# A squared-ReLU MLP in an encoder block: another order of units and column halves in the second product

## The chip, the cores and the metric

The kernel runs on one core of one Trainium2 chip. The metric is the device time of one execution in microseconds. Matrix work is done by TensorE (PE, with PEld for the loading of its stationary operand), elementwise work by VectorE (DVE) and ScalarE (ACT); GpSimd (POOL) has next to nothing to do here, and SyncE (SP) issues the transfers. PE writes into eight accumulation banks of 128 x 512 fp32 (PSUM).

## The reference

One encoder layer on 256 tokens of width 2048: an attention mixer, a cross-attention on 256 memory tokens, and an MLP of inner width 8192, each followed by a residual sum and a layer norm. Only the MLP is touched:

```python
def squared_relu_mlp(h, w_mlp_in, w_mlp_out):
    return jnp.square(jax.nn.relu(h @ w_mlp_in)) @ w_mlp_out

ff = squared_relu_mlp(x, w_mlp_in[l], w_mlp_out[l])
x = layer_norm(ALPHA * x + ff, ln3_g[l], ln3_b[l])
```

All of it is fp32. The kernel gets that precision from matmuls on two reduced halves of each operand: a number is split into hi and lo, and a product a*b is made as hi*hi + hi*lo + lo*hi, three matmuls (`mm3`).

## The kernel before, in words

**Chunks, tiles, units.** The inner width of 8192 is cut into four chunks c of 2048, and a chunk into 16 columns of 128. A *column tile* ("g", c, j) makes one column of 128 of the first product: 16 matmuls of 512 columns and 16 of 256 into one bank (`hidden_tile`). Its bank is then emptied (`evacuate`), and two tiles j, j+1 together form a pair p, which is squared and split into hi and lo in `ht` (`stages`). A *unit* ("u", c, q, p) multiplies pair p of chunk c with the rows of w_mlp_out that belong to it, for the column half q (1024 of 2048 columns), for both blocks of 128 tokens.

**Two kinds of units.** A unit is a 2 x 2 by 2 x 2 block product. A plain one takes eight block products, 24 matmuls of 512 columns, into the banks x11, x12, x21, x22. A unit in seven products (`sevens`) uses a Strassen-like scheme: 21 matmuls into p1, p5, p6, p7 and x11, x12, x21. For it DVE makes three sums of weight blocks into `s_t` (`push_sums`), and each pair's hidden values need sums as well (`add`, `halve_sums` in `stages`; kept in `aux`). x22 is free meanwhile and takes the tiles between such units. Each 1024 columns of weights (or of sums) are split by one copy on ACT and one subtraction on DVE (`part`); hi and lo have four buffers each.

**Passes.** A pass (c, q) is eight units. The passes run (0,0), (0,1), (1,0), (1,1) and so on; units 0 to 5 of each are in seven products, 6 and 7 plain, and the last pass is plain throughout. The four last units of the kernel are "held": their first token block is multiplied at once, the second after all weights have been split. The tiles of the second half of a chunk stand between the units of its first pass, the first half of the next chunk between those of its second pass, one tile ahead of each unit (two at one place). After the last seven-product unit of a pass p1, p5, p6, p7 are added into the residual `res` by way of `m_t`, and at its end x11, x12, x21, x22: 12 merges of 512 columns on DVE a pass (`merge`, `more`).

**What sets the order.** Matmuls, splits, sums and some other rows are recorded through `queue`, which makes each follow the one before on its engine. The merges and most of a pair's conversion are free rows, placed between them by a scheduler at build time. `after(n, ...)` hangs work behind the n-th coming split. The rows of ln2's gain and bias are applied to the residual by `norm_ops`: the first half of the columns beside the start of the chunk, the second half from the second pass on. Weights come in 1 MB loads through a ring of four buffers; from the load JOIN on `row_b`, which held those rows, is the fifth.

Lines that the prediction names: L962 and L961 are the split of 1024 columns on DVE and ACT (L958, L957 after the change), L954 the sums into `s_t`, L877 the emptying of a tile's bank, L881, L900, L903 and L904 the conversion of a pair, L1215 the norm rows (L1229 after), L1113, L1114 and L1117 the merges (L1118, L1119, L1122 after), L164 to L166 the three matmuls of `mm3`, L1035 and L1043 those of a tile (L1028, L1036 after), L1191 the last merges (L1205 after), L1254 and L1262 the output rows (L1266, L1274 after).

Of the kernel before, what the change touches and what calls it, by code (L numbers as in the profile page):

```python
# [18 lines left out]
P = 128  # L19
# [19 lines left out]
def encoder_kernel(ctx: ExitStack, tc: tile.TileContext, t, out):  # L39
# [808 lines left out]
    ht_x = aux[:, 0:1024].rearrange("p (k c) -> p k c", c=512)  # L848
    sums_h = [aux[:, o:o + 1024] for o in range(1024, 8192, 1024)]
# [5 lines left out]

    place, free = {}, {"h": list(range(SLOTS)), "s": list(range(len(SEVEN) + 1))}

# [6 lines left out]
    def hid(c, p):  # L864
        i = 2 * place["h", c, p]
        return ht[:, i:i + 2, :] if i < CH else ht_x[:, i - CH:i - CH + 2, :]
# [16 lines left out]
    def stages(h, c, p, to=free_order):  # L883

        a11, a21, a12, a22 = [h[:, o:o + P] for o in range(0, 4 * P, P)]
        s = []

        def square():
            to(nc.scalar.activation(h, h, AF.Relu))
            to(nc.scalar.activation(h, h, AF.Square))  # L890

        def halve():
            take("h", c, p)
            x = hid(c, p)
            ordered_split(x[:, :, 0:S], x[:, :, S:2 * S], h.rearrange("p (i c) -> p i c", c=S), to)

        def add():
            s.append(tmp_tile())
            s3, s1, s2, s4 = [s[0][:, o:o + P] for o in range(0, 4 * P, P)]
            to(nc.vector.tensor_tensor(out=s[0][:, 0:2 * P].rearrange("p (i c) -> p i c", c=P),  # L900
                                       in0=a21[:, None, :].broadcast_to([P, 2, P]),
                                       in1=h.rearrange("p (i c) -> p i c", c=P)[:, 0:4:3, :], op=ALU.subtract))
            to(nc.vector.tensor_tensor(out=s2, in0=s1, in1=a11, op=ALU.subtract))  # L903
# [7 lines left out]
        return [square, halve] + [add, halve_sums] * (p in SEVEN)  # L911

    raws, raw_of, fetched, sums = [raw_x], {}, [0], deque()
    items = []
    for c, q in PASSES:
        us = [("u", c, q, p) for p in ORDER]
        gs = [("g", c, j) for j in range(LEAD, CH)] if q == 0 else [
            ("g", c + 1, j) for j in range(LEAD) if c < NCH - 1]
        for u in us:
            n = 2 if q == 0 and u[3] == (CH // 2 - 2 if c else 0) else 1  # L920
            items += gs[:n] + [u]
            gs = gs[n:]
    JOIN = items.index(("u", 0, 1, 7))
# [92 lines left out]
    def both(*todo):  # L1016
        return [lambda: [x() for x in todo]]

    now, late_finish, later, count = [], [], [], [0]
# [7 lines left out]
    def hidden_tile(it, ps):  # L1027
# [23 lines left out]
        if first:  # L1051
            after(4, lambda: evacuate(ps, h, j % 2, queue))
        else:
            evacuate(ps, h, j % 2)
        if j % 2 and first:
            square, halve, add, halve_sums = stages(h, c, j // 2, queue)
            n = 11 if j == LEAD + 1 else 5
            after(n, square)
            after(n + 2, add, halve)
            after(n + 3, halve_sums)  # L1060
        elif j % 2:
            def rest():
                for stage in stages(h, c, j // 2, queue if j == CH - 1 else free_order):
                    stage()
            late_finish.append(rest)

    at = [0]

    def step():
# [3 lines left out]
        if it[0] == "g" and late_finish:  # L1073
            late_finish.pop()()
# [13 lines left out]
    def one_pass(c, q):  # L1088

        order, sevens = ORDER, SEVENS[c, q]  # L1090
        final = (c, q) == PASSES[-1]
# [3 lines left out]
        left = {id(ps): len(sevens) * (ps is not x22) + 2 * (len(order) - len(sevens)) for ps in xs}  # L1095
        left.update({id(ps): len(sevens) for ps in pt})
        left[id(x22)] -= 2 * HELD * final
        total = dict(left)
# [5 lines left out]

        cols = [slice((2 * q + i) * 512, (2 * q + i + 1) * 512) for i in range(2)]
        r11, r12, r21, r22 = [res[b][:, cc] for b in range(NB) for cc in cols]

        fresh = [r11, r12, r21, r22] if c == 0 else []
# [10 lines left out]
        spare, n_seven, n_unit, parts = [], 0, 0, []  # L1119
        while n_unit < len(order):  # L1120
            it = step()
            if it[0] == "g":  # L1122
                if n_unit == 0:
                    ps = {LEAD: x22, LEAD + 1: x21}[it[2]] if it[1] == 0 else p6
                elif n_seven < len(sevens):
                    ps = x22
                else:
                    spare = spare or [p1, p6]
                    ps = spare[0]
                    spare.reverse()  # L1130
                hidden_tile(it, ps)
# [3 lines left out]
            if p in sevens:  # L1135
                if n_seven == 0:
# [10 lines left out]
                n_seven += 1  # L1147
                if at[0] < len(items) and is_seven(items[at[0]]):
                    push_sums(items[at[0]])
                if n_seven == len(sevens):  # L1150
                    nc.scalar.activation(m_t, p1, AF.Copy)

                    banks.extend([lambda: merge(r11, m_t), lambda: more(p6),
                                  lambda: merge(r12, m_t, ALU.subtract), lambda: more(p7, ALU.subtract),
                                  lambda: merge(r21, m_t), lambda: merge(r22, m_t, ALU.subtract),
                                  lambda: merge(r22, p5), lambda: merge(r12, p5)])
            elif final and len(order) - n_unit < HELD:
                n = len(parts) // 2
                for i in range(2):
                    o = (2 * n + i) * 1024  # L1160
                    lo = sums_h[2 * n + i - 1] if n + i else lo_tile()
# [4 lines left out]
            else:  # L1166
                for i in range(2):
# [4 lines left out]
            if q == 1:  # L1172
                give("h", c, p)
                if p in SEVEN:
                    give("s", c, p)
            if late_finish:
                late_finish.pop()()
        if not final:
            for r, ps in ((r22, x22), (r12, x12), (r11, x11), (r21, x21)):
                merge(r, ps)  # L1180
            if c == NCH - 1:
                xs[:], pt[:] = pt[:], xs[:]
                banks.extend([lambda b=b, r=r: stats(sts[b], r)
                              for b, r in ((0, r11), (0, r12), (1, r21), (1, r22))])
            return
# [33 lines left out]
    for g in range(LEAD // G):  # L1219
# [4 lines left out]
        if g == 0:  # L1224
            norm_rows(0)
            rows = norm_ops(0)
            (a1, a2, a3, a4), (b1, b2, b3, b4) = first, second
            side.extend(wait * 4 + empty + [a1, b1, a3, a2, a4, b3] + both(b2, rows[0])
                        + both(b4, rows[1]) + rows[2:])  # L1229
# [153 lines left out]
```

## Time and profile before

| | |
|---|---|
| median of 3 runs | 1097.57 us (1096.83 to 1098.71) |
| the profiled execution's own time | 1098.32 us |
| its span (first to last instruction) | 1096.5 us |
| matmuls on PE | 5846 |
| first column tile of the queued part | 446.1 us |
| last matmul | ends at about 1085.5 us |

All rows are of this one execution. A row of a timeline gives start, duration, engine, line, operation, tiles and shape; behind it in brackets the idle time before it and what ended that. Durations overlap: an engine begins the next row before the last has drained, so the step from start to start is what a row costs on a full engine. Rows of windows give the stretch, its length, and for PE, PEld, DVE, ACT and POOL the busy time and the count; then the granted PE clock (1.00 is full), the share of the transfers and their GB/s. A row of waits gives who waited for whom, total us, times, longest us.

### The profile page before, as it was taken

The numbers are of one execution on the slowest core, as the hardware profiler recorded it, in microseconds if no ns is written. First come the engines' busy times: TensorE is split into PE (matmuls) and PEld (weight loads), VectorE is DVE, ScalarE is ACT, GpSimd is POOL, SyncE is SP. The second block draws the span as 40 slices with busy tenths as digits, with TensorE's granted clock in tenths as the row PEclk, the third lists the DMA queues.
The fourth block names the chain that finished last, engine by engine and source line by source line (L and its number), as shares of the span: only waits on it lengthen the run. The fifth ranks groups of instructions, "written<-read, shape, count | busy, mean of one in ns | idle before, by whom it ended". The sixth has DMA issues, their size and how long they took to land.

```text
span 1096.5 us, 15253 instructions
## 1 busy us (share of the span) xinstructions
PE 1076.7 (98%) x5846; PEld 928.8 (85%) x5846; DVE 938.7 (86%) x1301; ACT 642.3 (59%) x937; POOL 36.2 (3%) x43
## 2 busy tenths in 40 slices
PE   9999999999999999999999999999999999999995
PEld 6988899988999878878888888888888888888885
DVE  6878678778889677999999999899999899999876
ACT  6555567555576426656566557466566566666640
POOL 2402000000000000000000000000000000000000
PEclk9999999999999999999999999999999999999998
DMA  9664454466577334555556555646556555655732
GB/s 327 246 227 136 156 189 157 156 228 238 182 216 267 143 128 176 209 192 198 191 202 244 202 188 199 216 170 226 198 186 225 198 192 198 224 175 195 253 145 78
DMA packets 37369, 215.87 MB, mean 197 GB/s; under 512 B 4272, under 2 KB 5168, under 8 KB 13616
## 3 DMA queue, kind: packets, MB, share of 16 engines
q1 hardware_dynamic: 37296, 214.89, 55.5%
q8 instruction: 46, 0.75, 0.3%
q14 instruction: 27, 0.22, 0.1%
HBM read 212.78 MB, written 2.10 MB: 196 GB/s over the span
## 4 chain that ended last, share of the span: by engine, by line
PE 92%; DVE 6%; issue 1%; ACT 1%; DMA 1%; SPq 0%; POOL 0%; DVEq 0%; ACTq 0%
PE acc L164 12%; PE acc L165 12%; PE acc L166 12%; PE acc L1035 11%; PE att L1035 6%; PE acc L1043 6%; PE att L165 5%; PE att L166 5%; PE att L164 5%; PE att L1043 3%; PE acc L206 2%; PE acc L204 2%; PE acc L205 2%; DVE lo L962 2%; PE acc L213 1%; PE att L213 1%
## 5 line engine op out<-in xcount | busy, mean ns | idle before, releaser
L87 ACT ACTIVATE w_hi<-raw 128x1024 fp32r<-128x1024 f32 (+2 forms) x134 | 131.6, 989 | 108.5 <-PE acc L166 73.9
L88 DVE TENSOR_TENSOR w_lo<-raw,w_hi 128x1024 fp32r<-128x1024 f32 (+2 forms) x130 | 147.2, 1142 | 50.3 <-ACT w_hi L87 49.2
L962 DVE TENSOR_TENSOR lo<-raw,w_hi 128x1024 fp32r<-128x1024 f32 (+1 forms) x156 | 173.0, 1128 | 9.2 <-ACT w_hi L961 9.0
L961 ACT ACTIVATE w_hi<-raw 128x1024 fp32r<-128x1024 f32 (+1 forms) x156 | 149.3, 980 | 25.5 <-PE acc L166 15.0
L1035 PE MATMUL acc<-x2t,w_hi 128*128 128x512 f32 x592 | 153.3, 391 | 0.0
L1035 PEld LDWEIGHTS acc<-x2t,w_hi 128*128 128x128 f32 x592 | 108.9, 189 | 19.6
L962 DVE TENSOR_TENSOR lo<-s_t,w_hi 128x1024 fp32r<-128x1024 f32 x84 | 102.4, 1222 | 10.8 <-ACT w_hi L961 10.7
L961 ACT ACTIVATE w_hi<-s_t 128x1024 fp32r<-128x1024 f32 x84 | 88.6, 1057 | 37.3 <-PE acc L1035 18.4
L1043 PEld LDWEIGHTS acc<-x2t,lo 128*128 128x128 f32 x592 | 80.8, 190 | 5.8
L1043 PE MATMUL acc<-x2t,lo 128*128 128x256 f32 x592 | 82.5, 282 | 0.0
L1035 PE MATMUL att<-x2t,w_hi 128*128 128x512 f32 x304 | 78.4, 391 | 0.0
L165 PE MATMUL acc<-lo,ht 128*128 128x512 f32 (+1 forms) x188 | 73.0, 389 | 1.1 <-DVE lo L962 1.1
L164 PE MATMUL acc<-w_hi,ht 128*128 128x512 f32 x186 | 72.5, 390 | 0.0
L166 PE MATMUL acc<-w_hi,ht 128*128 128x512 f32 x186 | 72.4, 389 | 0.0
L876 ACT ACTIVATE tmp<-acc 128x256 f32<-128x256 f32 x41 | 15.4, 384 | 92.2 <-PE acc L1035 87.9
L165 PE MATMUL acc<-w_lo,xt 128*128 128x512 f32 (+2 forms) x192 | 69.3, 362 | 0.0
L166 PE MATMUL acc<-w_hi,xt 128*128 128x512 f32 (+2 forms) x192 | 69.2, 361 | 0.0
L164 PE MATMUL acc<-w_hi,xt 128*128 128x512 f32 (+2 forms) x192 | 65.6, 361 | 1.2 <-ACT w_hi L87 1.2
L1035 PEld LDWEIGHTS att<-x2t,w_hi 128*128 128x128 f32 x304 | 55.8, 189 | 10.0
L962 DVE TENSOR_TENSOR lo<-raw_x,w_hi 128x1024 fp32r<-128x1024 f32 (+1 forms) x50 | 55.4, 1124 | 0.6 <-ACT w_hi L961 0.4
L165 PE MATMUL att<-lo,aux 128*128 128x512 f32 x139 | 54.4, 391 | 1.4 <-DVE lo L962 1.4
L164 PE MATMUL att<-w_hi,aux 128*128 128x512 f32 x139 | 54.1, 390 | 0.0
(287 smaller groups left out, 2513.1 us busy)
## 6 DMA issues: line engine op xcount, KB each, us to landing
raw<-in_w_mo SPq DMA_DIRECT2D x39, 1024.0 KB, 4.8
raw<-in_w_mc SPq DMA_DIRECT2D x37, 1024.0 KB, 4.8
raw<-in_w_out SPq DMA_DIRECT2D x16, 1024.0 KB, 4.9
raw_x<-in_w_mo SPq DMA_DIRECT2D x14, 1024.0 KB, 4.8
raw_x<-in_w_mc SPq DMA_DIRECT2D x12, 1024.0 KB, 4.8
row_b<-in_w_mo SPq DMA_DIRECT2D x11, 1024.0 KB, 4.8
raw<-in_w_mi SPq DMA_DIRECT2D x8, 1024.0 KB, 4.8
row_b<-in_w_mc SPq DMA_DIRECT2D x7, 1024.0 KB, 4.8
```

Of the source, the lines that this page charges most:

```text
L87: pin(nc.scalar.activation(hi, src, AF.Copy), pinned)
L88: return pin(nc.vector.tensor_tensor(out=lo, in0=src, in1=f(hi), op=ALU.subtract), pinned)
L164: keep(nc.tensor.matmul(ps, ah, bh, start=start, stop=False))
L165: keep(nc.tensor.matmul(ps, ah, bl, start=False, stop=False))
L166: keep(nc.tensor.matmul(ps, al, bh, start=False, stop=stop))
L204: nc.tensor.matmul(ps, hi, xt[:, k, 0:S], start=k == 0, stop=False)
L205: nc.tensor.matmul(ps, hi, xt[:, k, S:2 * S], start=False, stop=False)
L206: nc.tensor.matmul(ps, lo, xt[:, k, 0:S], start=False, stop=k == nk - 1)
L961: queue(nc.scalar.activation(hi, src, AF.Copy))
L962: queue(nc.vector.tensor_tensor(out=lo, in0=src, in1=f(hi), op=ALU.subtract))
L1035: queue(nc.tensor.matmul(ps, hi[:, k * P:(k + 1) * P], x2t[:, k0 + k, :], start=k0 + k == 0, stop=k0 + k == KT - 1))
L1043: queue(nc.tensor.matmul(ps[:, 0:S], lo[:, k * P:(k + 1) * P], x2t[:, k0 + k, 0:S], start=False, stop=False))
```

## The change

The passes now run (0,0), (0,1), (1,1), (1,0), (2,0), (2,1), (3,1), (3,0): half 0, then two passes of half 1, two of half 0, two of half 1, and half 0. Two passes that follow each other on one half keep all their banks, and the merges come once for both. A table (`UNITS`) says which units are plain ("P") or in seven products ("S"), `ORDERS` in which order the pairs come, `TILES` how many column tiles stand before each unit. Plain units stand at the outer ends of such a double pass; there are 48 S and 16 P units (42 and 22 before). The first pass begins with four tiles around two plain units; after that one tile stands before each unit but two, none in the last pass, and the tiles run two further ahead than before. `ht` has eight places for pairs instead of nine, `aux` eight for sums instead of seven, and a pair is converted when a place is free (`finish`). Tiles between plain units take p1, p6 or p7 (`tile_bank`). The second half of the norm rows is applied in the first pass, and `row_b` joins the ring of weights earlier.

The first place is DVE from the third split of the column tiles on (lo_4182, lo_4183, lo_4180, lo_4181 are the four lo buffers). Before:

```order
L962 TENSOR_TENSOR lo_4182<-raw,w_hi 128x1024
L954 TENSOR_TENSOR s_t<-raw 128x1024
L962 TENSOR_TENSOR lo_4183<-raw,w_hi 128x1024
L954 TENSOR_TENSOR s_t<-s_t,raw 128x512 x2
L962 TENSOR_TENSOR lo_4180<-raw,w_hi 128x1024
L962 TENSOR_TENSOR lo_4181<-raw,w_hi 128x512
L900 TENSOR_TENSOR tmp<-tmp 128x256
L903 TENSOR_TENSOR tmp<-tmp 128x128
L904 TENSOR_TENSOR tmp<-tmp 128x128
L881 TENSOR_TENSOR ht<-tmp,ht 128x2x256
L877 TENSOR_TENSOR tmp<-acc,tmp 128x256
L962 TENSOR_TENSOR lo_4182<-s_t,w_hi 128x1024
```

And now:

```order
L958 TENSOR_TENSOR lo_4182<-raw,w_hi 128x1024
L958 TENSOR_TENSOR lo_4183<-raw,w_hi 128x1024
L958 TENSOR_TENSOR lo_4180<-raw,w_hi 128x1024
L877 TENSOR_TENSOR tmp<-acc,tmp 128x256
L958 TENSOR_TENSOR lo_4181<-raw,w_hi 128x1024
L900 TENSOR_TENSOR tmp<-tmp 128x256
L903 TENSOR_TENSOR tmp<-tmp 128x128
L904 TENSOR_TENSOR tmp<-tmp 128x128
L881 TENSOR_TENSOR ht<-tmp,ht 128x2x256
L1229 TENSOR_TENSOR res_1484<-res_1484,row_b 128x1024
L958 TENSOR_TENSOR lo_4182<-raw,w_hi 128x1024
L881 TENSOR_TENSOR aux<-tmp,aux 128x512
```

The sums of weight blocks (L954) have left this place, since the first two units are plain; a norm row (L1229) has come.

The second place is DVE where the second pass ends and the third begins. Before (res is the residual, att and acc are banks):

```order
L962 TENSOR_TENSOR lo_4181<-raw,w_hi 128x1024
L1113 SCALAR_TENSOR_TENSOR res_1485<-res_1485,m_t 128x512 x2
L962 TENSOR_TENSOR lo_4182<-row_b,w_hi 128x1024
L881 TENSOR_TENSOR aux<-tmp,aux 128x512
L1114 TENSOR_TENSOR res_1485<-res_1485,att 128x512
L1114 TENSOR_TENSOR res_1484<-res_1484,att 128x512
L962 TENSOR_TENSOR lo_4183<-row_b,w_hi 128x1024
L962 TENSOR_TENSOR lo_4180<-raw,w_hi 128x1024
L954 TENSOR_TENSOR s_t<-raw_x 128x1024
```

And now:

```order
L958 TENSOR_TENSOR lo_4183<-s_t,w_hi 128x1024
L958 TENSOR_TENSOR lo_4180<-raw,w_hi 128x1024
L950 TENSOR_TENSOR s_t<-raw 128x1024
L958 TENSOR_TENSOR lo_4181<-raw,w_hi 128x1024
L900 TENSOR_TENSOR tmp<-tmp 128x256
L950 TENSOR_TENSOR s_t<-s_t,raw 128x512
L881 TENSOR_TENSOR ht<-tmp,ht 128x2x256
L903 TENSOR_TENSOR tmp<-tmp 128x128
L950 TENSOR_TENSOR s_t<-s_t,raw 128x512
```

The merges are gone from here; the seven-product units of both passes follow each other, with one tile between (rows two to four and six to nine belong to a tile and the next unit's sums).

The third place is DVE at the end, from the last merge on. Before:

```order
L1191 TENSOR_TENSOR res_1485<-res_1485,acc 128x256
L524 BN_STATS bn<-res_1485 128x6 x2
L1191 TENSOR_TENSOR res_1485<-res_1485,acc 128x256
L524 BN_STATS bn<-res_1485 128x6
L528 BN_AGGR mv<-bn 128x2
```

And now:

```order
L1274 SCALAR_TENSOR_TENSOR res_1484<-res_1484,rs_r,raw 128x256
L524 BN_STATS bn<-res_1485 128x6
L1205 TENSOR_TENSOR res_1485<-res_1485,acc 128x256
L1274 SCALAR_TENSOR_TENSOR res_1484<-res_1484,rs_r,raw 128x256
L524 BN_STATS bn<-res_1485 128x6
L528 BN_AGGR mv<-bn 128x2
```

An output row of the first token block (L1274) has come between the last merge (L1205) and its statistics.

The diff, cut to its core:

```diff
-    SEVEN = (0, 1, 2, 3, 4, 5)
-    PASSES = [(c, q) for c in range(NCH) for q in range(2)]
-    ORDER = tuple(range(CH // 2))
-    SEVENS = {cq: SEVEN for cq in PASSES[:-1]}
-    SEVENS[PASSES[-1]] = ()
-    SLOTS = CH // 2 + 1
+    PASSES = [(c, (n + c) % 2) for c in range(NCH) for n in range(2)]
+    UNITS = ["PPSSSSSS", "PPSSSSSS", "SSSSSSSP", "PSSSSSSS", "SSSSSSSP", "PSSSSSSS", "SSSSSSPP", "PSPSPPPP"]
+    ORDERS = [(0, 1, 2, 3, 4, 5, 6, 7), (0, 1, 2, 3, 4, 5, 6, 7), (0, 1, 2, 3, 4, 5, 6, 7), (7, 0, 1, 2, 3, 4, 5, 6),
+              (0, 1, 2, 3, 4, 5, 6, 7), (7, 0, 1, 2, 3, 4, 5, 6), (0, 1, 2, 3, 4, 5, 6, 7), (7, 0, 6, 1, 2, 3, 4, 5)]
+    TILES = ["22111111", "11111111", "11111111", "11111111", "11111111", "10111111", "11111110", "00000000"]
+    SEVENS = {cq: [p for p, x in zip(o, u) if x == "S"] for cq, o, u in zip(PASSES, ORDERS, UNITS)}
+    SUMS = [set(SEVENS[c, 0] + SEVENS[c, 1]) for c in range(NCH)]
...
-    JOIN = items.index(("u", 0, 1, 7))
+    JOIN = items.index(("u", 0, 0, 4))
...
-            after(4, lambda: evacuate(ps, h, j % 2, queue))
+            after(3 if j == LEAD else 4, lambda: evacuate(ps, h, j % 2, queue))
...
+    def finish():
+
+        if late_finish and free["h"] and free["s"]:
+            h, c, p = late_finish.pop(0)
+            for stage in stages(h, c, p, queue if (c, p) == (NCH - 1, CH // 2 - 1) else free_order):
+                stage()
...
+        opens = n == 0 or PASSES[n - 1][1] != q
+        closes = final or PASSES[n + 1][1] != q
...
+        if opens:
...
+            whole = units if closes else units + UNITS[n + 1]
+            n_s, n_p = whole.count("S"), whole.count("P")
+            run["left"] = {id(ps): n_s + 2 * n_p for ps in (x11, x12, x21)}
+            run["left"].update({id(ps): n_s for ps in pt})
...
+        def tile_bank(it):
+
+            i = at[0] - 1
+            near = [[x for x in part_ if x[0] == "u"][:1] for part_ in (items[:i][::-1], items[i:])]
+            if all(x and is_seven(x[0]) for x in near) or it[1:] == (0, LEAD):
+                return x22
+            behind, ahead = [sum(x[0] == "g" for x in part_[:next(
+                (j for j, x in enumerate(part_) if is_seven(x) or x[1:] == (0, LEAD)), 0)])
+                for part_ in (items[:i][::-1], items[i + 1:])]
+            return p7 if behind == 1 and ahead else p6 if behind and not ahead else p1
...
-                if n_seven == len(sevens):
+                if run["s"] == 0:
                     nc.scalar.activation(m_t, p1, AF.Copy)
...
+                    xs_done = [lambda r=r, ps=ps: merge(r, ps) for r, ps in ((r12, x12), (r11, x11), (r21, x21))]
+                    banks.extend([lambda: merge(r11, m_t), lambda: more(p6)] + xs_done * (units[-1] == "S") + [
+                        lambda: merge(r22, p5), lambda: merge(r12, p5),
+                        lambda: merge(r12, m_t, ALU.subtract), lambda: more(p7, ALU.subtract),
+                        lambda: merge(r21, m_t), lambda: merge(r22, m_t, ALU.subtract)])
...
-    for cq in PASSES:
-        if cq == (0, 1):
-            for i, x in enumerate(norm_ops(1)):
-                after(6 * i + 8, x)
-        one_pass(*cq)
+    for i, x in enumerate(norm_ops(1)):
+        after(2 * i + 6, x)
+    for n in range(len(PASSES)):
+        one_pass(n)
```

More of the change, by code (lines that the diff above doesn't have):

```diff
@@ L909, in halve_sums @@
             ordered_split(y[:, 0, :], y[:, 1, :], s[0], to)
-        return [square, halve] + [add, halve_sums] * (p in SEVEN)
+        return [square, halve] + [add, halve_sums] * (p in SUMS[c])
     raws, raw_of, fetched, sums = [raw_x], {}, [0], deque()
     items = []
[L915 to L922, printed above, removed]
-    JOIN = items.index(("u", 0, 1, 7))
+    tiles = [("g", c, j) for c in range(NCH) for j in range(CH)][LEAD:]
+    for (c, q), order, counts in zip(PASSES, ORDERS, TILES):
+        for p, n in zip(order, counts):
+            items += [tiles.pop(0) for _ in range(int(n))] + [("u", c, q, p)]
+    JOIN = items.index(("u", 0, 0, 4))
     def fetch():
@@ L1014, in hidden_group @@
         return [lambda i=i, h=h: empty(i, h) for i, h in pairs], todo
-    def both(*todo):
-        return [lambda: [x() for x in todo]]
-    now, late_finish, later, count = [], [], [], [0]
+    now, late_finish, later, count, held_lo = [], [], [], [0], []
     def after(n, *todo):
@@ L1061, in hidden_tile @@
         elif j % 2:
[L1062 to L1065, printed above, removed]
+            late_finish.append((h, c, j // 2))
     at = [0]
+    def finish():
[3 more added lines that the diff above has]
+                stage()
     def step():
@@ L1086, in sm, with one_pass @@
         return x[:, 0, i * P:(i + 1) * P], x[:, 1, i * P:(i + 1) * P]
-    def one_pass(c, q):
-        order, sevens = ORDER, SEVENS[c, q]
-        final = (c, q) == PASSES[-1]
+    run = {}
+    def one_pass(n):
+        c, q = PASSES[n]
+        final, units, sevens = n == len(PASSES) - 1, UNITS[n], SEVENS[c, q]
+        opens = n == 0 or PASSES[n - 1][1] != q
+        closes = final or PASSES[n + 1][1] != q
         if final:
@@ L1094, in one_pass @@
         (x11, x12, x21, x22), (p1, p5, p6, p7) = xs, pt
[L1095 to L1098, printed above, removed]
+        if opens:
+            cols = [slice((2 * q + i) * 512, (2 * q + i + 1) * 512) for i in range(2)]
+            r11, r12, r21, r22 = run["res"] = [res[b][:, cc] for b in range(NB) for cc in cols]
+            whole = units if closes else units + UNITS[n + 1]
+            n_s, n_p = whole.count("S"), whole.count("P")
+            run["left"] = {id(ps): n_s + 2 * n_p for ps in (x11, x12, x21)}
+            run["left"].update({id(ps): n_s for ps in pt})
+            run["left"][id(x22)] = 2 * (n_p - HELD) if final else 2 * (len(whole) - len(whole.lstrip("P")))
+            run["total"] = dict(run["left"])
+            run["fresh"] = [r11, r12, r21, r22] if c == 0 else []
+            run["s"] = run["sevens"] = n_s
+        r11, r12, r21, r22 = run["res"]
+        left, total, fresh = run["left"], run["total"], run["fresh"]
         def mm(ps, x, hi, lo):
@@ L1117, in more @@
             nc.vector.tensor_tensor(out=m_t, in0=m_t, in1=ps, op=op)
-        spare, n_seven, n_unit, parts = [], 0, 0, []
-        while n_unit < len(order):
+        def tile_bank(it):
[7 more added lines that the diff above has]
+            return p7 if behind == 1 and ahead else p6 if behind and not ahead else p1
+        n_unit, parts = 0, []
+        while n_unit < len(units):
             it = step()
             if it[0] == "g":
[L1123 to L1131, printed above, removed]
+                hidden_tile(it, tile_bank(it))
                 continue
@@ L1135, in one_pass @@
             if p in sevens:
-                if n_seven == 0:
+                if run["s"] == run["sevens"] and not final:
                     while banks:
@@ L1226, in encoder_kernel @@
             rows = norm_ops(0)
-            (a1, a2, a3, a4), (b1, b2, b3, b4) = first, second
-            side.extend(wait * 4 + empty + [a1, b1, a3, a2, a4, b3] + both(b2, rows[0])
-                        + both(b4, rows[1]) + rows[2:])
+            (a1, a2), (b1, b2) = first, second
+            side.extend(wait * 4 + empty + [a1, b1, a2, b2] + rows)
             s_in.split, s_in.beside = queued_split, 2
```

52 lines of the change are left out of this document (25 added, 27 removed).

## The prediction

> **What bounds the kernel now.** I read the page's head first, then the windows of the second MLP product, then the waits and the timeline inside it.
>
> ```profile
> span 1096.5 us, 15253 instructions
> PE 1076.7 (98%) x5846; PEld 928.8 (85%) x5846; DVE 938.7 (86%) x1301; ACT 642.3 (59%) x937; POOL 36.2 (3%) x43
> ...
> 466.00:496.00 30.00, 26.99 (x133) 21.49 (x132) 28.69 (x40) 18.93 (x27) 0.00 (x0) 1.00 0.56 193
> 496.00:560.00 64.00, 64.00 (x325) 54.62 (x324) 60.26 (x72) 38.55 (x49) 0.00 (x0) 1.00 0.56 200
> 560.00:584.00 24.00, 22.90 (x117) 18.72 (x116) 23.96 (x30) 14.95 (x20) 0.00 (x0) 1.00 0.55 204
> 584.00:640.00 56.00, 56.00 (x285) 47.70 (x285) 52.46 (x69) 34.10 (x45) 0.00 (x0) 1.00 0.61 220
> 640.00:840.00 200.00, 200.00 (x1024) 171.13 (x1023) 188.37 (x237) 126.97 (x165) 0.00 (x0) 1.00 0.56 200
> ```
>
> In a window row the stretch's length is followed by the busy time of PE, PEld, DVE and ACT. From 584 us on PE never stops: there only fewer matmuls can shorten the path. In two short stretches PE does stop (26.99 of 30, 22.90 of 24), and just there DVE is full (28.69 and 23.96). The waits of 447 to 600 us name the cause, the timeline shows one, and two holds too short to leave any or much idle time:
>
> ```profile
> PE att L165 <- DVE lo L962: 2.9, 5, 0.8
> PE acc L165 <- DVE lo L962: 1.1, 1, 1.1
> ...
> 470.52 0.39 PE L164 MATMUL att<-w_hi,aux 128*128 128x512 f32 x1
> 470.91 0.50 PE L165 MATMUL att<-lo,aux 128*128 128x512 f32 x1
> ...
> 491.75 0.39 PE L164 MATMUL acc<-w_hi,ht 128*128 128x512 f32 x1
> 493.19 0.50 PE L165 MATMUL acc<-lo,ht 128*128 128x512 f32 x1 [1.06 <-DVE lo L962]
> ...
> 560.96 0.40 PE L164 MATMUL att<-w_hi,ht 128*128 128x512 f32 x1
> 561.48 0.50 PE L165 MATMUL att<-lo,ht 128*128 128x512 f32 x1
> ...
> 639.70 0.39 PE L165 MATMUL att<-lo,aux 128*128 128x512 f32 x1
> 639.93 0.39 PE L166 MATMUL att<-w_hi,aux 128*128 128x512 f32 x1
> ...
> 641.52 1.98 PE L1035 MATMUL acc<-x2t,w_hi 128*128 128x512 f32 x8
> 643.33 1.12 PE L1043 MATMUL acc<-x2t,lo 128*128 128x256 f32 x8
> 644.28 0.40 PE L1035 MATMUL acc<-x2t,w_hi 128*128 128x512 f32 x1
> ```
>
> A matmul's 0.39 overlaps the next one, so its price is the step from start to start: from 639.70 eight 512-wide matmuls take 1.82 us, 0.2275 each; the eight 256-wide ones take 0.95, 0.119 each. So a unit in seven products (21 matmuls) costs PE 4.78 us, a plain one (24) 5.46, a column tile (16 wide, 16 narrow) 5.55. A hold loses more than its idle time: 491.75 to 493.19 is 1.44, 1.21 over the step, with 1.06 shown idle. Six waits of 4.0 us in all, with 0.16 each, are 5.0; the short holds at 470.52 (0.39) and 560.96 (0.52) add 0.16 and 0.29. **PE loses about 5.4 us to late lo halves, all in the first chunk.**
>
> The same way for DVE, in the steady stretch, with three rows of the first chunk that part 3 uses:
>
> ```profile
> 444.95 2.35 DVE L962 TENSOR_TENSOR lo<-raw_x,w_hi 128x1024 fp32r<-128x1024 f32 x2
> ...
> 639.76 1.23 DVE L962 TENSOR_TENSOR lo<-row_b,w_hi 128x1024 fp32r<-128x1024 f32 x1 [0.24 <-ACT w_hi L961]
> 640.91 1.22 DVE L954 TENSOR_TENSOR s_t<-raw 128x1024 f32<-128x1024 f32 x1
> 642.04 0.42 DVE L900 TENSOR_TENSOR tmp<-tmp 128x256 f32<-128x256 f32 x1
> 642.38 1.22 DVE L962 TENSOR_TENSOR lo<-row_b,w_hi 128x1024 fp32r<-128x1024 f32 x1
> 643.51 0.69 DVE L954 TENSOR_TENSOR s_t<-s_t,raw 128x512 f32<-128x512 f32 x1
> 644.12 0.29 DVE L903 TENSOR_TENSOR tmp<-tmp 128x128 f32<-128x128 f32 x1
> 644.32 0.69 DVE L881 TENSOR_TENSOR ht<-tmp,ht 128x512 fp32r<-128x512 f32 x1
> ...
> 568.76 1.22 DVE L1215 TENSOR_TENSOR res<-res,row_b 128x1024 f32<-128x1024 f32 x1
> ...
> 447.92 1.12 PE L1043 MATMUL acc<-x2t,lo 128*128 128x256 f32 x8
> ```
>
> Start to start: 1024 columns 1.14, 512 columns 0.60, 256 columns 0.34, 128 columns 0.20. A seven-product unit asks of DVE three splits and one half split (4.02) and the sums into s_t (1.14 + 2 x 0.60): 6.36 us. A plain unit asks 2.28, a tile 2.28 + 0.34 for emptying its bank, and half of a pair's conversion (0.34 + 2 x 0.20 + 2 x 0.60 = 1.94): 0.97. So tile and seven-product unit need 9.95 of DVE in 10.33 of PE, tile and plain unit 5.87 in 11.01. The first kind only just fits; the second gives DVE 5.1 us to catch up.
>
> **Part 1, fewer matmuls.** Seven-product units go from 42 to 48, plain ones from 22 to 16. Each exchange takes three 512-wide matmuls away: 18 x 0.2275 = **4.1 us** off a PE that is always busy there. The column tiles stay 56.
>
> The Trainium skill ("TensorE: Matmul & The Clock Gate", the section on 56 against 53.3 ns in Part 1) gives a step of N / 2.4 GHz + 2.5 ns, 215.7 ns at 512 columns. By it this term would be an estimated 3.9 us. The trace's step of 227.5 ns is longer, and the sum goes by the trace.
>
> **Part 2, DVE's work, in all.** Counted over both orders: twelve more rows of 1024 columns (six splits net, six sums), five fewer of 512 (20 more from splits, sums and the two extra pair conversions, 25 fewer merges, because banks are emptied once per two chunks), two more of 256 and four of 128: 13.7 - 3.0 + 0.7 + 0.8 = 12.2 us more. They cost nothing if they lie under PE: in 640 to 840 us DVE is idle for 11.6 of 200, about 36 over the whole product. ACT gets six copies of 1024 and some eight of 512 more; it is busy for 127 of those 200. If that cover were gone, all 12.2 would be on the path. So what matters is where they stand.
>
> **Part 3, the first chunk.** The first tile's first lo is written from 444.95 to about 446.17 and read at 447.92: a lead of 1.75. From there to the 25th split (in the third unit) the order before has 24 rows of 1024, 20 of 512, 13 of 256 and 8 of 128: 45.38 us of DVE against 42.54 of PE. The lead is spent 1.1 us short even if DVE never waits. So the holds of 466 to 496 follow from the order. In the changed order the first two units are plain, with four tiles before and between them, and pairs 0 and 1 have no sums. To the 18th split (the end of the first seven-product unit) it has 21 rows of 1024, 11 of 512, 13 of 256 and 8 of 128: 36.56 us against 40.49, a lead of 5.7. To the 48th, the end of the pass, 86.54 against 92.15. DVE is nowhere behind, although four norm rows of 1.14 now lie here. They lay in the second pass before (L1215), where 22 splits ask 41.82 of DVE against 39.28 of PE, so that the holds of 560 to 584 come out too. The same units now ask 52.20 against 55.99 over 32 splits. **Both groups of holds go: 5.4 us.** Bounds: 0, if something other than DVE's queue sets them, and 5.4; I take 5.4, since the sums reproduce where the holds were.
>
> **Part 4, the long runs.** Banks kept over two chunks make runs of 13 and 14 seven-product units with no plain one between. In the first run (76 splits) the rows sum to 126.16 of DVE against 128.81 of PE, so the lead does not shrink. At the plain units where a run ends, up to 13 merges (7.8 us) stand against 2 x 5.1. The price is nothing while the cover of 0.38 a unit holds.
>
> **Part 5, banks and queues.** The tiles at a run's end now take p1, p7 and p6 in turn, and p7 is free only after the second addition into m_t. In DVE's order that row stands right behind the split for the second half of the tile that wants the bank. The split's lo buffer comes free when the tile before ends, one plain unit (5.46) ahead; then follow a copy on ACT, the split (1.14) and the addition (0.60).
>
> ```profile
> L961 ACT ACTIVATE w_hi<-raw 128x1024 fp32r<-128x1024 f32 (+1 forms) x156 | 149.3, 980 | 25.5 <-PE acc L166 15.0
> ```
>
> With 0.98 for the copy 2.7 us remain. Behind this row wait the next unit's splits, and PE behind them. SP issues the same 120 weight loads; its row_b loads begin earlier, behind the norm rows. Price: 0 to 1.5 us at each of four run ends, if something of the size of such a copy and a half comes between; I take 0, because of the 2.7.
>
> **Part 6, the tail.** The last rows in the trace:
>
> ```profile
> 1085.20 0.28 PE L166 MATMUL acc<-wide,ht 128*128 128x256 f32 x1
> ...
> 1085.52 0.42 DVE L1191 TENSOR_TENSOR res<-res,acc 128x256 f32<-128x256 f32 x1 [1.40 <-PE acc L166]
> 1085.97 0.43 DVE L524 BATCH_NORM_STATS2 bn<-res 128x6 f32<-128x256 f32 x1
> ...
> 1090.14 0.48 DVE L1254 SCALAR_TENSOR_TENSOR res<-res,mv,s_t 128x256 f32<-128x256 f32 x1
> 1090.54 0.75 DVE L1262 SCALAR_TENSOR_TENSOR res<-res,rs_r,raw 128x512 f32<-128x512 f32 x1
> ```
>
> In the changed order one 256-wide output row stands between the last L1191 and the statistics: 1090.14 to 1090.54, **0.4 us later**. In the last pass two seven-product units come without tiles, each asking 1.58 more of DVE than of PE; the plain units about them give back 3.2 each, so nothing more is charged.
>
> **The sum.** -4.1 - 5.4 + 0.4 = -9.1. The profiled execution took 1098.32 (span 1096.5), and would take 1089.2; it lies 0.75 above the median, so the median goes from 1097.57 to **1088.5**.
>
> **Rivals.** (a) *Only the matmuls count.* The early holds stay or move, because the copies of ACT that DVE waits for are late too. For it: DVE itself was held in that stretch (0.24 in the row at 639.76 is such a wait). Against: windows full of DVE. 1097.57 - 4.1 + 0.4 = 1093.9. (b) *A bank released late* at the four run ends, 1.5 each: 1088.5 + 6.0 = 1094.5; against it, DVE's lead. (c) *The last pass.* If the lead is spent when the first unit without a tile comes, PE waits 2 x 1.58: 1091.7. For it: ends of runs leave DVE little lead; against: two plain units stand just before. (d) *DVE bounds the long runs,* the slower side. A unit with its tile has 0.38 to spare; with waits for ACT of 0.24 twice it is short by 0.10, with four by 0.58. Over 40 such units that is 23 us: 1088.5 + 23 = 1111.5. It decides from 1.6 waits a unit on. Against it: 640 to 840 us has runs of six without any PE idle. (e) *The change doesn't do what it says,* so that merges come as often as before: excluded by the rows, 25 fewer.
>
> **Chances.** Forecast 0.72, (a) 0.08, (b) 0.05, (c) 0.08, (d) 0.07. What a measurement here can tell from no change is about 0.2%, 2.2 us. All but (d) are faster than that; (d) in its milder forms gives no change. Faster 0.93, same 0.03, slower 0.04. Range: below, 1.5 for holds not counted; above, to just short of (a), with (c) inside: 1087.0 to 1092.0.
>
> **What would show it.** In the windows of the product PE is busy throughout, from its first tile on, with no wait on lo; DVE is busy some 96% in the long runs; PE has 5828 matmuls. If PE waits on lo inside the long runs, part 4 was wrong; if in the first two passes, part 3; if waits at PE name m_t or res, part 5; if L1205's last row starts as late after the last matmul as now, but the end comes over 0.6 later after it, part 6.

## The result, and the profile after

The changed kernel takes **1086.87 us** (median, 1085.92 to 1088.06) against 1097.57: 10.70 us less, a ratio of 0.9901 (95% interval 0.9886 to 0.9915). The forecast was 1088.5, 9.1 less, with a range of 1087.0 to 1092.0. The direction and the mechanism held; the gain was 1.6 us larger than the sum, and the time lies 0.13 us under the range. The profiled execution took 1086.87 us.

The head of the page of the changed kernel, and the windows of the product, with the same columns as before:

```profile
span 1085.1 us, 15274 instructions
PE 1069.8 (99%) x5828; PEld 925.4 (85%) x5828; DVE 948.0 (87%) x1314; ACT 651.3 (60%) x949; POOL 37.3 (3%) x43
...
466.00:496.00 30.00, 30.00 (x160) 25.86 (x159) 26.26 (x37) 16.69 (x23) 0.00 (x0) 1.00 0.58 212
...
560.00:584.00 24.00, 24.00 (x122) 20.48 (x121) 20.37 (x27) 15.95 (x21) 0.00 (x0) 1.00 0.51 175
640.00:840.00 200.00, 200.00 (x1025) 171.15 (x1024) 191.59 (x241) 130.67 (x171) 0.00 (x0) 1.00 0.57 203
```

PE has 5828 matmuls, 18 fewer, and is busy through both stretches in which it stopped before: 160 matmuls in 466 to 496 us where there were 133 (a part of that is another mix of wide and narrow ones). DVE has 13 rows more and is 96% full in 640 to 840 us, and PE still runs through. All waits of PE that the trace names are these five, and none lies in the product:

```profile
PE acc L213 <- ACT x2t L757: 1.6, 1, 1.6
PE acc L128 <- DVE ones L121: 1.1, 1, 1.1
PE att L752 <- DVE res L740: 0.7, 1, 0.7
PE acc L165 <- DVE w_lo L88: 0.6, 1, 0.6
PE acc L164 <- ACT w_hi L87: 0.3, 1, 0.3
```

The steps from start to start show one operand that came just in time and left no idle time. It lies in the second seven-product unit of the last pass:

```profile
1038.79 0.39 PE L164 MATMUL acc<-w_hi,aux 128*128 128x512 f32 x1
1039.09 0.50 PE L165 MATMUL acc<-lo,aux 128*128 128x512 f32 x1
1039.42 0.39 PE L166 MATMUL acc<-w_hi,aux 128*128 128x512 f32 x1
```

The steps are 0.30 and 0.33 where 0.23 is usual, together 0.2 us. No other pair of steps in the product looks like this.

To see where the 10.7 us went, take the product from its first column tile to the start of its last matmul, which for the kernel before is the row at 1085.20 that the prediction quotes. The starts of the product in both timelines, before first, and the changed kernel's tail:

```profile
446.11 0.85 PE L1035 MATMUL acc<-x2t,w_hi 128*128 128x512 f32 x3
...
1091.59 0.88 DVE L1262 SCALAR_TENSOR_TENSOR res<-res,rs_r,raw 128x256 f32<-128x256 f32 x2
```

```profile
444.98 0.62 PE L1028 MATMUL acc<-x2t,w_hi 128*128 128x512 f32 x2
...
1073.88 0.28 PE L166 MATMUL acc<-wide,ht 128*128 128x256 f32 x1
1074.20 0.42 DVE L1205 TENSOR_TENSOR res<-res,acc 128x256 f32<-128x256 f32 x1
1074.54 0.48 DVE L1274 SCALAR_TENSOR_TENSOR res<-res,rs_r,raw 128x256 f32<-128x256 f32 x1
1074.93 0.42 DVE L524 BATCH_NORM_STATS2 bn<-res 128x6 f32<-128x256 f32 x1
1080.55 0.87 DVE L1274 SCALAR_TENSOR_TENSOR res<-res,rs_r,raw 128x256 f32<-128x256 f32 x2
```

| | before | after | difference |
|---|---|---|---|
| ahead of the product | 446.11 | 444.98 | -1.13 |
| product, to the start of its last matmul | 639.09 | 628.90 | -10.19 |
| from the start of the last matmul to the end of DVE's last row | 7.27 | 7.54 | +0.27 |
| from the end of DVE's last row to the end of the span | 4.0 | 3.7 | -0.3 |

The two profiled executions differ by 11.45 us. The 1.13 ahead of the product stand where the program was not changed; the last two experiments bear on them. The change itself is the second row and the third, with the 0.3 to the end of the span behind them.

### The profile page after: what moved, and what is told of

Read it like the earlier page. It is cut to its first block, busy times and chain, and to the rows that moved or that the text cites. A ratio compares the mean times of both kernels' runs of the same rounds, so it can differ in the third digit from the quotient of the medians.

```text
span 1085.1 us, 15274 instructions
## 1 busy us (share of the span) xinstructions
PE 1069.8 (99%) x5828; PEld 925.4 (85%) x5828; DVE 948.0 (87%) x1314; ACT 651.3 (60%) x949; POOL 37.3 (3%) x43
## 4 chain that ended last, share of the span: by engine, by line
PE 93%; DVE 3%; DMA 2%; issue 1%; ACT 0%; SPq 0%; POOL 0%; DVEq 0%; ACTq 0%
PE acc L1028 15%; PE acc L165 12%; PE acc L164 12%; PE acc L166 12%; PE acc L1036 8%; PE att L164 5%; PE att L166 5%; PE att L165 5%; PE att L1028 4%; PE acc L206 2%; PE acc L204 2%; PE acc L205 2%; PE att L1036 2%; PE acc L213 1%; PE att L213 1%; DMA raw<-in_w_qa 1%
## 5 line engine op out<-in xcount | busy, mean ns | idle before, releaser
L1028 PE MATMUL acc<-x2t,w_hi 128*128 128x512 f32 x688 | 178.4, 391 | 0.0
L1028 PEld LDWEIGHTS acc<-x2t,w_hi 128*128 128x128 f32 x688 | 126.6, 189 | 22.8
L958 DVE TENSOR_TENSOR lo<-s_t,w_hi 128x1024 fp32r<-128x1024 f32 x96 | 117.1, 1220 | 15.1 <-ACT w_hi L957 14.9
L957 ACT ACTIVATE w_hi<-s_t 128x1024 fp32r<-128x1024 f32 x96 | 101.5, 1057 | 42.5 <-DVE lo L958 18.7
L1036 PEld LDWEIGHTS acc<-x2t,lo 128*128 128x128 f32 x688 | 93.9, 190 | 6.7
L1036 PE MATMUL acc<-x2t,lo 128*128 128x256 f32 x688 | 95.9, 282 | 0.0
L165 PE MATMUL acc<-lo,ht 128*128 128x512 f32 x174 | 67.7, 389 | 0.0
L166 PE MATMUL att<-w_hi,aux 128*128 128x512 f32 x140 | 54.5, 389 | 0.0
L164 PE MATMUL att<-w_hi,aux 128*128 128x512 f32 x140 | 54.5, 389 | 0.0
L1028 PE MATMUL att<-x2t,w_hi 128*128 128x512 f32 x208 | 53.9, 392 | 0.0
L165 PE MATMUL acc<-w_lo,ot 128*128 128x512 f32 (+1 forms) x136 | 51.7, 381 | 0.0
```

The costliest lines, as they stand in the source:

```text
L164: keep(nc.tensor.matmul(ps, ah, bh, start=start, stop=False))
L165: keep(nc.tensor.matmul(ps, ah, bl, start=False, stop=False))
L166: keep(nc.tensor.matmul(ps, al, bh, start=False, stop=stop))
L957: queue(nc.scalar.activation(hi, src, AF.Copy))
L958: queue(nc.vector.tensor_tensor(out=lo, in0=src, in1=f(hi), op=ALU.subtract))
L1028: queue(nc.tensor.matmul(ps, hi[:, k * P:(k + 1) * P], x2t[:, k0 + k, :], start=k0 + k == 0, stop=k0 + k == KT - 1))
```

## The experiments

All are set against the changed kernel's 1086.87 us. The kernel before was run beside them twice more, with medians of 1097.62 and 1097.51 where it had 1097.57, so the times can be compared.

**Undo part 1: 42 seven-product units in the changed order.**

```diff
-    UNITS = ["PPSSSSSS", "PPSSSSSS", "SSSSSSSP", "PSSSSSSS", "SSSSSSSP", "PSSSSSSS", "SSSSSSPP", "PSPSPPPP"]
+    UNITS = ["PPSSSSSS", "PPPSSSSS", "SSSSSSPP", "PPSSSSSS", "SSSSSSPP", "PPSSSSSS", "SSSSSPPP", "PSPSPPPP"]
```

> The changed kernel with six of its 48 seven-product units turned back to plain ones (the unit next to the plain ones at an end of six passes), so that 42 and 22 are left, as in the kernel before; passes, kept banks and column tiles stay as changed. PE then has 5846 matmuls, as before. Theory (part 1: every exchange costs three 512-wide matmuls on a PE that is always busy): 18 x 0.2275 = +4.1 us over the changed kernel, about 1091.0, with no wait for a lo half in the product. Rival (the gain came from the order and the kept banks alone, and the exchanged matmuls were hidden in other losses): within 1 us of the changed kernel. Second rival (what was missed in the forecast's size lies in the exchange, which also takes merges and copies away): +5 to +6 us.

Measured: 1091.59 us (1091.06 to 1093.56), +4.7. In its timeline the product runs from and to these rows:

```profile
445.13 0.62 PE L1028 MATMUL acc<-x2t,w_hi 128*128 128x512 f32 x2
...
1078.09 0.28 PE L166 MATMUL acc<-wide,ht 128*128 128x256 f32 x1
```

That is 632.96 us, 4.06 over the changed kernel, or 0.226 for each of the 18 matmuls; its waits show none for a lo half. So part 1 is 4.1, as forecast. And since this kernel has as many matmuls as the one before, their difference of 639.09 - 632.96 = **6.1 us is what the order and the kept banks bring by themselves**, where the forecast had 5.4. The medians say the same: 1097.62 - 1091.59 = 6.0. So 0.7 of the sum's error is in that term.

**Undo part 3: seven-product units first.** The first pass has its plain units at its end, and the lead is one tile shorter; the tile comes back in the sixth pass. The rest follows from that and is not in these lines (the second tile goes into x21, and the stages of the early pairs, now with sums, are queued in another order).

```diff
-    UNITS = ["PPSSSSSS", ...
+    UNITS = ["SSSSSSPP", ...
-    TILES = ["22111111", "11111111", "11111111", "11111111", "11111111", "10111111", "11111110", "00000000"]
+    TILES = ["21111111", "11111111", "11111111", "11111111", "11111111", "11111111", "11111110", "00000000"]
```

> The changed kernel with the two plain units of the first pass moved from its start to its end and one tile of the lead taken away, so that seven-product units with sums come at once, as in the kernel before; the number of matmuls stays that of the changed kernel. Theory (part 3: the early holds are DVE's queue in the first chunk, and the plain units at the outer end take them away): counted over its order DVE falls up to 4.5 us behind PE by the 23rd split of the first pass, against a lead of 1.75 at the first; PE waits again for lo halves between about 455 and 500 us, 2.8 us in all if DVE never waits itself and up to 7.8 if it does, so 1089.7 to 1094.7. Rival (the holds came from the later passes or from ACT's copies, not from the place of the sums): no waits for lo in the first pass, 1086 to 1088.

Measured: 1096.83 us (1095.02 to 1098.77), +10.0 with the same 5828 matmuls. That is 2.1 over the highest time expected. Its waits of 446 to 560 us, then its timeline with the product's ends and one hold:

```profile
PE att L165 <- DVE lo L958: 4.3, 4, 1.8
PE acc L165 <- DVE lo L958: 1.1, 1, 1.1
PE acc L164 <- DVE tmp L877: 0.7, 1, 0.7
```

```profile
447.05 0.62 PE L1028 MATMUL acc<-x2t,w_hi 128*128 128x512 f32 x2
...
469.90 0.40 PE L164 MATMUL att<-w_hi,ht 128*128 128x512 f32 x1
472.10 0.50 PE L165 MATMUL att<-lo,ht 128*128 128x512 f32 x1 [1.81 <-DVE lo L958]
472.44 0.39 PE L166 MATMUL att<-w_hi,ht 128*128 128x512 f32 x1
472.67 0.39 PE L164 MATMUL acc<-w_hi,aux 128*128 128x512 f32 x1
...
1084.03 0.28 PE L166 MATMUL acc<-wide,ht 128*128 128x256 f32 x1
```

The product takes 636.98 us, 8.1 more, and it starts 2.1 later than in the changed kernel's profile; the clock, below, is 1.5 of that. Seven holds between 462 and 500 us are over the step by 7.2 us in all, inside the expected 2.8 to 7.8. Six of them are for a lo half. The seventh, of 0.9, is for the emptying of a tile's bank (L877), which is DVE's work too. The other 0.8 is in the rows shown: after the hold at 472.10 the next matmul starts 0.34 later, not 0.23, and only then does the step return to 0.23. That is 0.11 at each of seven holds. The theory stands, and shows what the forecast's price of a hold left out. How much of the holds is due to the sums and how much to the missing tile was not separated.

**The second group of holds: the kernel before, without four norm rows.**

```diff
-        if cq == (0, 1):
-            for i, x in enumerate(norm_ops(1)):
-                after(6 * i + 8, x)
```

> The kernel before, without the second half of its norm rows (gain and bias of the first norm on columns 1024 to 2047 of the residual are left out, four DVE rows of 1.14 us in the second pass). Theory (part 3, second group: the holds of 560 to 584 us are DVE's queue, 41.82 of DVE against 39.28 of PE): without 4.56 us of DVE work there the holds at 560 to 584 are gone and those at 466 to 496 stay; 1.6 to 2.2 us less than the kernel before, about 1095.5. Rival (a hold there comes from ACT or a load): the holds stay, 1097 to 1098.

Measured: 1096.51 us (1093.79 to 1097.45), a median 1.1 under the 1097.62 of the kernel before, less than the expected 1.6 to 2.2; ratio 0.9982 (0.9973 to 0.9991). The granted clock over the whole span blurs the times: it was 0.995 to 0.997 here and 0.994 to 0.997 there. The executions with 0.997 alone have medians of 1095.26 (four) and 1097.17 (seven), 1.9 apart. The profile is clearer. Its windows, then the ends of its product in the timeline:

```profile
466.00:496.00 30.00, 27.14 (x129) 21.81 (x130) 28.72 (x38) 20.42 (x28) 0.00 (x0) 1.00 0.54 203
560.00:584.00 24.00, 24.00 (x122) 20.48 (x121) 23.67 (x30) 17.08 (x23) 0.00 (x0) 1.00 0.63 219
```

```profile
443.96 0.62 PE L1035 MATMUL acc<-x2t,w_hi 128*128 128x512 f32 x2
1081.05 0.28 PE L166 MATMUL acc<-wide,ht 128*128 128x256 f32 x1
```

PE is busy through 560 to 584 us, the first group stays, and the product takes 637.09 us, 2.0 less, inside the expected 1.6 to 2.2. These holds were DVE's queue.

**How near is DVE to its bound? One more row in each seven-product unit,** of 256 columns, and in a second kernel of 512.

```diff
+        last = sums.pop()
+        sums.append(lambda: [last(), queue(nc.vector.tensor_tensor(
+            out=s_t[:, 1536:1792], in0=s_t[:, 1024:1280], in1=raw[:, 1536:1792], op=ALU.add))])
```

> The changed kernel with one DVE row of 256 columns (0.34 us) more in each of its 48 seven-product units: a part of the last sum into s_t is written a second time. PE's work stays the same. A seven-product unit with its tile had 0.38 us of DVE to spare by part 4. Theory (the reserve is 0.38 and the lead is not eaten): 0.34 is under it, so PE still never waits in the long runs; 0 to +2 us over the changed kernel, the 2 for units whose tile's neighbour also carries merges, 1087 to 1089. Rival (the real reserve is smaller, because DVE itself waits for ACT's copies, as in rival d): several waits for lo in each run, above +4.

> The same with 512 columns (0.60 us) in each seven-product unit. Theory: 0.60 - 0.38 = 0.22 is missing in each of 48 units, 10.6 us in all, less what the lead at the start of a run pays: in the changed kernel's trace the shortest lead of a lo half inside a run is 0.86 us, four units' worth, in four or five runs, so +7 to +10.6 and 1094 to 1097.5, with waits for lo through all long runs. Rival (DVE is nowhere near a bound, the lead pays for all): under +2.

Measured: 1093.31 us (1092.16 to 1094.3) with 256 columns, +6.4; 1099.37 (1098.66 to 1102.57) with 512, +12.5. Both are above what was expected, and with 256 columns the theory of a reserve of 0.38 in every unit falls. First the window with 256 columns:

```profile
640.00:840.00 200.00, 199.89 (x1016) 169.04 (x1015) 195.47 (x255) 131.41 (x168) 0.00 (x0) 1.00 0.58 200
```

The PE column looks full, 199.89 of 200, yet 9 matmuls fewer were done in the same time. Only the steps show why:

```profile
676.02 1.21 DVE L961 TENSOR_TENSOR lo<-s_t,w_hi 128x1024 fp32r<-128x1024 f32 x1
...
676.98 0.39 PE L164 MATMUL att<-w_hi,aux 128*128 128x512 f32 x1
677.28 0.50 PE L165 MATMUL att<-lo,aux 128*128 128x512 f32 x1
677.62 0.40 PE L166 MATMUL att<-w_hi,aux 128*128 128x512 f32 x1
```

The split of this lo half ends at 677.23 and is read at 677.28: just in time. PE is not shown idle, but the step into that matmul is 0.30 and the next one 0.34. There are 21 late or just-in-time rows, from 505.19 to 1042.72 us; their steps average 0.35 and 0.34, so they cost 21 x (0.12 + 0.11) = 4.8 of the 5.2 us by which the product grew (to 634.12). With 512 columns the product takes 641.16 us, 12.3 more. There are 36 such rows, whose own steps are over by 7.3 us in all and the steps behind them by 3.9. The 7.3 lies inside the expected 7 to 10.6; it is again the late step behind a hold that the expectation left out.

Inside the runs they come every 20.9 us, that is in every second unit: the one in which a pair's conversion (1.94) falls. The prediction spread this over two units. Taken apart, such a unit asks DVE for 10.92 in 10.33 of PE and the other for 8.98; with the added 0.34 the first is 0.93 short. The shortest lead of a lo half in the changed kernel from 640 to 700 us is 0.86, in units of both kinds, so what the light unit saves does not carry over. Near the start of a run the lead is shorter than the expectation took it to be: the lo half that is done at 591.78 us is read at 592.37, 0.59 later. That four lo buffers cap the lead is my reading; no run had a fifth.

The reserve is there, then, but it is the lead of 0.86 at the heavy unit and not 0.38 on average. The time is the rival's (above +4), but its cause is only in part: DVE does wait for ACT's copies, above all ahead of the splits of s_t, while PE is late only in the heavy units. This is that group in the changed kernel, and behind it the same group with 256 columns more:

```profile
L958 DVE TENSOR_TENSOR lo<-s_t,w_hi 128x1024 fp32r<-128x1024 f32 x96 | 117.1, 1220 | 15.1 <-ACT w_hi L957 14.9
```

```profile
L961 DVE TENSOR_TENSOR lo<-s_t,w_hi 128x1024 fp32r<-128x1024 f32 x96 | 116.8, 1218 | 5.3 <-ACT w_hi L960 4.2
```

Of 15.1 us of idle time ahead of these splits the added rows, 16 us in all, filled 10, and PE already paid. Whether a faster ACT would give DVE room was not tested.

**One seven-product unit more.** The third pass becomes "SSSSSSSS".

> The changed kernel with one more seven-product unit, the last of the third pass, so that 49 and 15 are left and one plain unit stands between two runs there. PE has three 512-wide matmuls less (0.7 us). Theory (DVE's catching up needs both plain units: a run's end brings merges of up to 7.8 us, two plain units give 2 x 5.1 and one gives 5.1): the 0.7 us are lost again to waits for lo or to a late bank at that place, -0.3 to +1.5 against the changed kernel. Rival (PE's matmuls alone count): -0.7.

Measured: 1089.07 us (1087.4 to 1089.75), +2.2. The product takes 629.13 us, 0.2 more, in spite of 0.7 us of matmuls less. One wait for a lo half is long enough to be named:

```profile
736.44 0.50 PE L165 MATMUL att<-lo,ht 128*128 128x512 f32 x1 [0.27 <-DVE lo L958]
```

It stands in the second seven-product unit behind the single plain one, behind the run's merges and a pair's conversion on DVE, and costs 0.44 in its own step and 0.11 in the next. So the 0.7 us are lost again as the theory said, and the exchange gains nothing at this place; others were not tried. Most of the 2.2 lies outside the product: its first column tile starts at 446.18 in this profile, 1.2 later than in the changed kernel's, and that is the clock, below. The remaining 0.8 is not explained.

**PE's gap ahead of the product, filled and widened.** First eight matmuls of ones fill the gap; then, in another kernel, ACT repeats one conversion and widens it.

```diff
+        if beside is not None:
+            for _ in range(8):
+                pin(nc.tensor.matmul(outs[0], ones, ones[:, None, :].broadcast_to([P, 4, P]),
+                                     start=True, stop=True), True)
```

```diff
-                gain2(x2t[:, k, 0:S], ps[:, o], k, True)
+                for _ in range(5 if k == 0 else 1):
+                    gain2(x2t[:, k, 0:S], ps[:, o], k, True)
```

> The changed kernel with eight more 512-wide matmuls of ones, into a bank that the next real product starts anew, in the gap of PE of about 1.6 us just before the first column tiles of the product (397 us). In the profile of before the granted clock was 0.66 in the 4 us behind that gap, in that of the changed kernel 1.00, and the first column tile starts 1.1 us earlier in the latter, although the program up to there is the same. Theory (the clock falls after PE's gaps in some executions, and costs some 1.1 to 1.4 us then): the granted clock is 1.00 at 396 to 404 us in this kernel, and its time is 0 to 1.2 us under that of the changed kernel, with its runs closer together. Rival (the two profiles differ by something else, or the gap is not what lowers the clock): the clock falls here in some executions as well, no gain; the dummy matmuls may cost up to 0.5 us where they reach over the gap's end.

> The changed kernel with PE's gap before the first column tiles made longer: ACT writes the first quarter row of the transposed residual four times more (0.56 us less overlap each, about 1.7 to 2.2 us in all), and nothing else. Theory (the granted clock falls after this gap in some executions, because PE's idle time there is just about what lowers it): with a gap of some 3.4 us it falls in nearly every execution, so that the granted clock is under 0.95 in the 4 us behind the gap, and the time is 1.7 to 2.2 + about 1.2 = 2.9 to 3.4 us over the changed kernel. Rival (the clock's fall at this place does not hang on the gap's length): +1.7 to +2.2, the clock low in the same minority of executions as before.

Measured: filled, 1086.82 us (1086.12 to 1087.26), no gain that can be told; widened, 1091.53 (1090.58 to 1093.68), +4.7. Windows behind the gap, before, after and widened (the third number from the end is the granted clock), with the widened gap's own row:

```profile
396.00:400.00 4.00, 2.48 (x8) 2.13 (x8) 3.28 (x7) 1.86 (x4) 0.00 (x0) 0.66 0.00 0
400.00:404.00 4.00, 4.00 (x24) 3.55 (x24) 1.51 (x3) 1.20 (x4) 0.00 (x0) 0.92 0.47 130
```

```profile
396.00:400.00 4.00, 2.43 (x14) 1.95 (x13) 3.09 (x7) 1.82 (x4) 0.00 (x0) 1.00 0.00 0
400.00:404.00 4.00, 4.00 (x27) 3.60 (x26) 2.77 (x7) 1.98 (x4) 0.00 (x0) 1.00 0.40 115
```

```profile
396.00:400.00 4.00, 0.17 (x2) 0.00 (x0) 0.97 (x2) 3.25 (x6) 0.00 (x0) 0.70 0.00 0
400.00:404.00 4.00, 3.88 (x11) 3.33 (x12) 3.27 (x7) 1.14 (x3) 0.00 (x0) 0.50 0.00 0
404.00:408.00 4.00, 4.00 (x25) 3.48 (x25) 1.32 (x3) 1.65 (x3) 0.00 (x0) 0.94 0.82 215
```

```profile
400.12 2.04 PE L213 MATMUL acc<-x2t,wide 128*128 128x512 f32 x4 [3.96 <-ACT x2t L757]
```

The same place with the gap as it is, before and after:

```profile
395.29 0.66 PE L752 MATMUL att<-ident,res 128*128 128x128 f32 x4 [0.72 <-DVE res L740]
397.51 2.04 PE L213 MATMUL acc<-x2t,wide 128*128 128x512 f32 x4 [1.57 <-ACT x2t L757]
```

```profile
397.79 1.16 PE L213 MATMUL acc<-x2t,wide 128*128 128x512 f32 x4 [1.57 <-ACT x2t L757]
```

With the gap as it is, the clock fell in four of eight profiles: the kernel before, the one with seven-product units first, the one with 512 columns and the one with 49 units. What a fall costs can be read from the start of this L213 to the first column tile. That takes 48.6 to 48.7 us in those four profiles (397.51 to 446.11 in the kernel before) and 47.1 to 47.2 in the other four and in the one with the gap filled (397.79 to 444.98 in the changed kernel). So a fall costs 1.4 to 1.5 us. Of the 1.13 us ahead of the product 1.41 are the clock's; the changed kernel's gap ended 0.28 later.

With the gap widened the same stretch takes 49.1 us. The granted clock over the whole span was 0.993 in each of five executions (0.995 to 0.997 in the changed kernel's), so the clock seems to fall there every time. Of the 4.7 us 2.4 are the longer gap, and 1.9 the slower clock. That is more than the expected 1.2: the fall is twice as long, and a part of it lies in the gap itself.

With the gap filled the clock did not fall in the one profile, which says little alone, since it did not fall in half of the others either. So it is the widened gap that bears the theory out. That filling the gap gains time is not shown: the median is the same as the changed kernel's, whose profile has no fall, and its four executions lie within 1.1 us where the changed kernel's five lie within 2.1.

## What the prediction had right, and the step that failed

- **Part 1** (4.1): right; 4.06 in the product when it alone is undone. The rule of the Trainium skill ("TensorE: Matmul & The Clock Gate", the section on 56 against 53.3 ns in Part 1) gave an estimated 3.9; the measured 0.226 a matmul lies at the trace's step of 0.2275. The trace agrees with that rule for other matmuls: the eight bf16 ones that fill the gap step 0.216 (from 395.38 to 397.11 us).
- **Part 2** (12.2 us of DVE's work, hidden): the 13 rows more are there, and no wait came of them but the 0.2 us at 1039 us.
- **Part 3** (5.4): the mechanism was right. Both groups of holds are gone. The first group comes back when the seven-product units come first, and in the kernel before the second goes with four norm rows. **Its size is the step that failed.** The forecast priced a hold by the step into the held matmul alone, but the matmul behind it is late too. In the kernel before, behind the hold at 493.19 that the prediction quotes:

```profile
493.53 0.40 PE L166 MATMUL acc<-w_hi,ht 128*128 128x512 f32 x1
493.76 0.40 PE L164 MATMUL att<-w_hi,aux 128*128 128x512 f32 x1
494.93 0.50 PE L165 MATMUL att<-lo,aux 128*128 128x512 f32 x1 [0.77 <-DVE lo L962]
495.27 0.40 PE L166 MATMUL att<-w_hi,aux 128*128 128x512 f32 x1
```

  From 493.19 to 493.53 and from 494.93 to 495.27 are 0.34; from 493.53 to 493.76 the step is 0.23 again. Eight holds give 8 x 0.11 = 0.9, and 5.4 + 0.9 = 6.3. The forecast had none left after the change, and 0.2 are left (at 1039 us); 6.3 - 0.2 are the 6.1 that stand between the two kernels with 5846 matmuls, of which the one in the changed order has the same 0.2, at 1043 us.
- **Part 4** (0): right for this kernel, and rival (d) did not come, but the reason given was too comfortable. The cover is not 0.38 in each unit: 0.34 more already costs 5.2 us in the product.
- **Part 5** (0): right; no wait in the product names m_t, res or a bank.
- **Part 6** (+0.4): the row stands where it was said, at 1074.54; to the end of DVE's last row it costs 0.27. That no more was charged for the last pass was 0.2 short: the operand at 1039 us belongs to one of its two seven-product units without tiles, where rival (c) had put a loss of up to 3.2.
- **The sum**, with the measured terms, is -4.1 - 6.1 + 0.3 = -9.9. The span behind DVE's last row is 0.3 shorter, which nothing in the forecast covers and no run explains: -10.3 with the unrounded rows. The medians lie 10.7 apart. The other 0.4 is under what a measurement here can tell. The clock would account for it, as far as a few executions show: those whose granted clock was 0.997 have medians of 1097.17 (nine of the kernel before, from its two later series) and 1086.87 (three of the changed kernel), 10.3 apart.
- **The range** left 1.5 below for holds not counted. The holds took 0.7 of it and the tail 0.1. With the 0.3 at the end of the span and the 0.4 of the clock, for which the forecast had no term, the time came to lie 0.13 under it.

## What to carry to other kernels

Price a hold on PE by the steps on both sides of it, and look for holds in the steps and in matmuls per window, not in busy time: an operand that comes just in time leaves no idle row and still costs some 0.2 us here, in its own step and the next. Where work alternates between heavy and light units, compare the engines unit by unit and with the lead that the buffers allow, not on average. An engine that sets the pace in the first units of a stage can be relieved by moving cheap units to that place; the new order was worth more here (6.1 us) than the matmuls saved (4.1).

## What the hardware showed that was not expected

PE's granted clock falls behind two short gaps, the waits for res and x2t of 0.7 and 1.6 us shown above with 0.7 us of transposes (L752) between them, in some profiles and not in others of kernels with the same code there. The windows give the length: (0.34 + 0.08) x 4 us = 1.68 us of full clock lost before, that is 3.4 us at half clock; with the gap of 3.96 us, (0.30 + 0.50 + 0.06) x 4 = 3.44 us, twice as long. The 0.50 is the window that lies in the fall as a whole. The Trainium skill ("TensorE: Matmul & The Clock Gate", the section on what's actually happening in Part 1) describes a free-running window of about 3.4 us; one idle window halves the clock. The trace agrees in the length and the half, and a window that runs freely would explain why the same gaps lower the clock only sometimes. The Trainium skill's advice on that page, in the section on why this matters for your kernels, is to leave no gap over some 3 us. No gap here was longer than 1.6 us, and the clock still fell. Only the second gap was widened and filled; what the first one adds, and whether the transposes between them count as work for the clock, no run here shows.

The other finding is the step after a just-in-time operand: 0.33 to 0.34 us instead of 0.23, in every hold quoted here, from 0.07 over the step (676.98 to 677.28) to 2.0 (469.90 to 472.10). Why the next matmul is late was not tested.
